# A hybrid decoder layer on one core: projection tiles in the order queries, delta rule, keys, values, pooling, gate, and half of the cached keys multiplied beside the delta rule's tiles

## Chip, cores and metric

One core of a Trainium2 chip. The metric is the device time in microseconds (us) of one execution. Engines: TensorE (PE), VectorE (DVE), ScalarE (ACT), GpSimd (POOL) and SyncE (SP); SP, ACT and POOL also issue DMAs, each in its own program order.

## What is computed

One inference step of a layer with four head groups: A (gated delta rule), B (RWKV-7 time mixing), C (forgetting attention) and D (causal pooling), for a prompt of 1024 tokens and 8 single decode tokens with a cache of 4096 positions each. Cut to its frame:

```python
def _layer(x, start_pos, st, past, P):
    proj = jnp.einsum('ntd,de->nte', x, P['w_in'])
    qkv_A, a_A, b_A, z_A, p_B, z_B, qkv_C, f_C, z_C, u_D, z_D = _split_proj(proj)
    o_A, conv_n, S_A_n = _gdn_branch(qkv_A, a_A, b_A, ...)        # chunks of 64, triangular solve, scan
    o_B, shift_n, S_B_n = _rwkv7_branch(p_B, ...)                 # scan
    o_C, k_n, v_n, lf_n = _fox_branch(qkv_C, f_C, ..., past)      # softmax(q k/8 + decays) v, over the cache too
    o_D, pool_n = _pool_branch(u_D, ...)
    gated = concatenate([o_A*silu(z_A), o_B*silu(z_B), o_C*silu(z_C), o_D*silu(z_D)])
    out = jnp.einsum('nte,ed->ntd', gated, P['w_out'])
    y = _layernorm(ALPHA_DN * x + out, P['ln_g'], P['ln_b'])
```

## The kernel before, in words

**Projection.** The 7,200-odd input columns are cut into 57 tiles of 128 columns. Tile names: MISC; BT (16 tiles of B, the last of each four its gate); AT (16 of A, likewise); CQ, CK, CV, CZ (queries, keys, values, gate of C, four each); DU, DZ (input and gate of D, four each). `self.seq` lists the tiles in the order in which they are multiplied; before it is MISC, BT, AT, CQ, DU, DZ, CK, CV, CZ. `project` computes one tile with 144 matmuls of 344 columns (float32 split in a high and a low part) into three PSUM banks tagged `pj`, of which there are only three, so the next tile starts when ACT has copied the previous one out (`stg<-pj`, L365). Weights arrive by DMA as `raw`; ACT makes `whi`, DVE `wlo`.

**Fillers.** All other work is written as generators. `project` calls `fill` four times for each tile; a call lets every registered generator advance by its rate (counted in `yield`s), and `drain` runs what is left once the tiles are used up. A scheduler with its own cost table then fixes the order of instructions on every engine; on the chip each engine keeps that order.

**Stages.** `inputs` multiplies MISC and BT beside B's preparation, then AT beside A's preparation (`prep_a`, rate 1.6) and `start_b` (triangular inverses of B, decode step of B; rate 1). `inputs_cd` multiplies the last 24 tiles beside two generators:

- `cached` (rate 1.6): inverses of A, `decode_k` (scores of the 8 decode tokens against 32 pages each of cached keys: 64 MB on SP's DMA queue as 256 issues of 256 KB into tiles `dkv`, 1024 small matmuls `k<-dkv,dqb`, L997), and `decode_softmax`.
- `recurrent` (rate 1.0): `chain_b` and `chain_a` (16 chunks each, one `yield` a chunk), then, once the last DZ tile is there, `branch_d` (8 yields), `post_chain_b` (16 yields), then, once the cached softmax and the last CK tile are done, `setup_late` (constants, read through a tile `late` of the stage pool) and `c_first`: for attention heads 1 and 0 it loads queries and keys and finds the row maxima of the scores (`c_max`: 12 matmuls `a<-ckx,cqm` with a mask each, 12 DVE reductions `cmx<-a` into 8 columns, L785 to L799; the maxima go through a small DMA `cmr<-cml` back to partitions of `cqx`, L832).

The pool `stage2` of `inputs_cd` has two buffers `stg`. A CZ tile uses both: one for the projected tile, one as scratch for its silu (L1204 to L1212, three DVE and three ACT passes of 1032 columns). `branch_d` does a silu of the same size for each of its four groups.

**After the projection** `mixing` runs attention for 8 heads (`s`, `cpt`, `cph`, `cpl`, `v`) with the cached values (`decode_v`) as filler, then the output projection (`o`) and the norm.

Of the kernel before, what the change touches and what calls it, by code (L numbers as in the profile page):

```python
# [17 lines left out]
N = T + NS  # L18
G3 = 344
GROUPS = (392, 384, 256)  # L20
RATE_R = 1.0
EARLY = (1,)
RATE_P = 1
SPOOL = {0: 99, 1: 99, 2: 0}
# [15 lines left out]
MISC, CQ, CK, CV, CZ, DU, DZ, BT, AT = 0, 1, 5, 9, 13, 17, 21, 25, 41  # L40
# [139 lines left out]
class Kernel:  # L180
# [732 lines left out]
        nc.gpsimd.dma_start(self.G[8 + hp, :, :T], num)  # L913


    def pages(self, pool, bufs, lead):

        tiles = {}

        def load(n):  # L920
            t = tiles[n] = self.t(pool, [128, 1024], "dkv", bufs=bufs)
            c, b = divmod(n, 8)
            src, view = self.I["ck"], t.rearrange("p (j h k) -> p j (h k)", j=2, h=4)
            for j in range(2):
                v = self.page(32 * b + 2 * c + j, src.shape[0])
                s = src[bass.ds(v, 1)].rearrange("a p h k -> (a p) (h k)")
                self.paged.append(self.nc.sync.dma_start(view[:, j], s))

        def get(n):
            for m in range(n, min(n + lead + 1, 128)):  # L930
                if m not in tiles:
                    load(m)
            return tiles[n]
        return get
# [17 lines left out]
            return tiles[n]  # L952
        return get

    def decode_k(self, **side):


        nc, I, O = self.nc, self.I, self.O
        pj, lf = O["pj"], self.lfd
        with self.tc.tile_pool(name="dqk", bufs=1, **side) as pool:  # L960
            qs = self.t(pool, [128, 4, 8], "dqs")
            nc.gpsimd.dma_start(qs, pj[CQ:CQ + 4, :, T:].rearrange("t p b -> p t b"))
            qb = self.t(pool, [128, 4, 8, 32], "dqb")
            nc.gpsimd.memset(qb, 0.0)
            qf = qb.rearrange("p h b m -> p h (b m)")
            for hh in range(2):
                r = slice(64 * hh, 64 * hh + 64)
                nc.vector.tensor_copy(qf[r, :, 8 * hh::33][:, :, 0:8], qs[r])
            get = self.pages(pool, 3, 2)
            get(0)  # L970
            yield True
            carry = None
            for c in range(16):
                if c % 2 == 0:

                    cum = self.t(pool, [128, 1 + 512], "dcum")
                    nc.gpsimd.memset(cum, 0.0)
                    for hp in range(4):
                        for hh in range(2):
                            r = slice(32 * hp + 8 * hh, 32 * hp + 8 * hh + 8)  # L980
                            h = 2 * hp + hh
                            nc.gpsimd.dma_start(cum[r, 1:].rearrange("p (g k) -> p g k", k=128),
                                              lf[:, 2 * c:2 * c + 4, 128 * h:128 * h + 128])
                            if c == 0:
                                nc.gpsimd.dma_start(cum[r, 0:1], O["lf"][h, T:].unsqueeze(1))
                    if c:
                        nc.vector.tensor_copy(cum[:, 0:1], carry)
                    nc.vector.tensor_tensor_scan(cum[:, 1:], self.onec.to_broadcast([128, 512]), cum[:, 1:],
                                                 cum[:, 0:1], ALU.mult, ALU.add)
                    carry = self.t(pool, [128, 1], "dcar", bufs=2)  # L990
                    nc.vector.tensor_copy(carry, cum[:, 512:513])
                    s = self.t(pool, [128, 512], "dso")
                ps = self.ps("k", (128, 256))
                for b in range(8):
                    kt = get(8 * c + b).rearrange("p (j h k) -> p j h k", j=2, h=4)
                    for hp in range(4):
                        nc.tensor.matmul(ps[32 * hp:32 * hp + 32], lhsT=qb[:, hp, b], rhs=kt[:, :, hp],  # L997
                                         start=b == 0, stop=b == 7)
                    if b % 2 and b < 7:
                        yield True  # L1000
                o = 256 * (c % 2)
                nc.vector.scalar_tensor_tensor(s[:, o:o + 256], ps, 0.125, cum[:, o:o + 256], op0=ALU.mult, op1=ALU.add)
                if c % 2:
                    nc.gpsimd.dma_start(self.sco[:, 512 * (c // 2):512 * (c // 2) + 512], s)
                yield True
            while CK + 3 not in self.done:
                yield True

            ks = self.t(pool, [128, 4, 8], "dks")
            nc.gpsimd.dma_start(ks, pj[CK:CK + 4, :, T:].rearrange("t p b -> p t b"))  # L1010
            ps = self.ps("k")
            for hp in range(4):
                for b in range(8):
                    nc.tensor.matmul(ps[32 * hp:32 * hp + 32, 0:1], lhsT=qb[:, hp, b], rhs=ks[:, hp, b:b + 1],
                                     start=b == 0, stop=b == 7)
            s0 = self.t(pool, [128, 1], "ds0")
            nc.scalar.activation(s0, ps[:, 0:1], AF.Copy, scale=0.125)
            nc.gpsimd.dma_start(self.sco[:, 4096:4097], s0)
# [732 lines left out]
    def build(self):  # L1751
        tc, nc = self.tc, self.nc
        P = lambda **k: tc.tile_pool(reuse_waits="tile", **k)
# [14 lines left out]
        w = lambda t: [self.I["w"][t][:, 4 * k:4 * k + 4] for k in range(4)]  # L1768
        four = lambda t: list(range(t, t + 4))
        prep = lambda t: [t + 4 * h + i for h in (0, 1) for i in range(4)] + [t + 8, t + 9, t + 10, t + 12, t + 13, t + 14, t + 11, t + 15]  # L1770
        self.seq = [MISC] + prep(BT) + prep(AT) + four(CQ) + four(DU) + four(DZ) + four(CK) + four(CV) + four(CZ)
        with P(name="const", bufs=1) as cp, P(name="psum", bufs=2, space=PSUM) as self.psum0:
            with P(name="psum1", bufs=2, space=PSUM) as self.psum1:
                with P(name="w", bufs=2) as wp, P(name="x", bufs=1) as xp:
# [16 lines left out]
            with P(name="psum2", bufs=2, space=PSUM) as self.psum1:  # L1791
                R = dict(side="right")
                with P(name="wo", bufs=2, **R) as wp, P(name="ost", bufs=2, **R) as sp, P(name="y", bufs=1, **R) as yp, \
# [4 lines left out]
                    with P(name="g1", bufs=1) as g1:  # L1798
                        g = [self.gated(3, g1, sp)]
                        with P(name="posta", bufs=1) as pp:  # L1800
                            post = self.post_chain_a(pp)
# [18 lines left out]
    def inputs(self, cp, sp):  # L1820

        P = lambda **k: self.tc.tile_pool(reuse_waits="tile", **k)
        R = dict(side="right")
        raw = self.post_raw(sp)
        ps = [[self.ps(x, (128, G3)) for x in y] for y in (("pj",) * 3, "aab")]
        self.first(self.seq[0:2], ps)
        with self.tc.high_priority(offset=AHEAD):
            raw(MISC, ps[0])()
        lx = self.lora_inputs(sp)
        with P(name="rows", bufs=1, **R) as rp:  # L1830
            self.rows(rp)
        with P(name="bprep", bufs=1, **R) as bp:
            pb = self.post_b(sp, bp, 1.6)
            with self.tc.high_priority(offset=AHEAD):
                pb(self.seq[1], ps[1])
            self.lora(cp, bp, *lx)
            for t in self.seq[2:17]:
                self.project(t, raw if (t - BT) % 4 == 3 else pb)
            self.drain()
        with P(name="aprep", bufs=1, **R) as ap:  # L1840
            self.decay_columns(sp)
            self.cached_gates(sp)
            pa = self.post_a(sp, ap, 1.6)
            self.add(self.start_b(), 1)
            for t in self.seq[17:33]:
                self.project(t, raw if (t - AT) % 4 == 3 else pa)
            self.drain()

    def inputs_cd(self, sp):
        R = dict(side="right")  # L1850
        raw = self.post_raw(sp)
        self.stage2 = sp
        self.add(self.cached(), RATE_L)
        self.add(self.recurrent(**R), RATE_R)
        for t in self.seq[33:]:
            self.project(t, raw)
        self.drain()

    def start_b(self):

        yield from self.inverses("B")
        with self.tc.tile_pool(reuse_waits="tile", name="smpB", bufs=1) as pool:
            yield from self.sample_b(pool)

    def cached(self):
        yield from self.inverses("A")
        self.done.add("invA")
        while CQ + 3 not in self.done:
            yield 1
        yield from self.decode_k()  # L1870
        yield from self.decode_softmax()
        self.done.add("decK")

# [18 lines left out]
    def recurrent(self, **side):  # L1892

        P = lambda **k: self.tc.tile_pool(reuse_waits="tile", bufs=1, **side, **k)
        yield from self.chain_b(**side)
        while "invA" not in self.done:
            yield 1
        yield from self.chain_a(**side)
        while DZ + 3 not in self.done:
            yield True  # L1900
        with P(name="d") as pool:
            yield from self.branch_d(pool)
        with P(name="post") as pool:
            yield from self.post_chain_b(pool)
        while "decK" not in self.done or CK + 3 not in self.done:
            yield 1
        self.c0 = self.tc.tile_pool(reuse_waits="tile", name="c0", bufs=1, **side)
        pool = self.c0.__enter__()
# [24 lines left out]
```

## Time and profile before

| | us |
|---|---|
| median of three runs (2424.43 to 2431.7) | 2431.46 |
| the profiled execution | 2431.75 |
| its span, first to last instruction | 2430.0 |
| PE busy in the span | 2330.0 (96%) |
| DVE busy | 1371.7 (56%) |
| ACT busy | 940.3 (39%) |

The table's last rows are sums over stages that are limited by different things, so they say little alone; the rows further down are cut by stage. In these, "PEclk" is the share of TensorE's full clock that was granted, and idle time of an engine has behind it what ended it.

### The profile page before, as it was taken

How to read it: one execution, taken by the hardware profiler on the slowest of the kernel's cores; microseconds unless marked ns; L12 is line 12 of the kernel's file. 1: busy time of each engine (PE TensorE's matmuls, PEld its weight loads, DVE VectorE, ACT ScalarE, POOL GpSimd, SP SyncE). 2: the span in 40 equal slices, each digit the busy share in tenths (PEclk: the TensorE clock that was granted, in tenths of full speed). 3: DMA queues.
4: the chain of work that ended last, by engine and by line, in shares of the span. 5: the costliest groups of instructions: out<-in, count | busy, mean ns of one | idle time of the engine just before them, and what ended most of it. 6: DMA issues, size and time to landing. Idle time of an engine off the chain costs nothing. (4 is left out here: it accounts for less than half of the span.)

```text
span 2430.0 us, 48607 instructions
## 1 busy us (share of the span) xinstructions
PE 2330.0 (96%) x18324; PEld 2055.6 (85%) x18324; DVE 1371.7 (56%) x2677; ACT 940.3 (39%) x1861; POOL 298.8 (12%) x416
## 2 busy tenths in 40 slices
PE   8999999999999999999999999999999989999984
PEld 8999999999988999897777777999855579878984
DVE  4665667777465567522222244554588654564598
ACT  5644445434443444221111122553466665201244
POOL 0000000000000000112112111100122110100175
PEclk9999999999999999999999999999999999999997
DMA  6233433545432345878888888553398785783312
GB/s 215 52 107 88 111 87 93 150 92 111 109 79 66 92 105 127 181 191 259 268 266 280 278 282 300 187 159 79 111 277 240 230 299 161 216 299 116 91 65 87
DMA packets 368388, 401.46 MB, mean 165 GB/s; under 512 B 203853, under 2 KB 227326, under 8 KB 367386
## 3 DMA queue, kind: packets, MB, share of 16 engines
q1 hardware_dynamic: 306418, 262.78, 36.8%
q10 hardware_dynamic: 50056, 101.60, 14.9%
q0 software_dynamic: 11680, 33.99, 4.1%
q8 instruction: 144, 2.36, 0.4%
q14 instruction: 90, 0.74, 0.1%
HBM read 314.56 MB, written 83.62 MB: 164 GB/s over the span
## 5 line engine op out<-in xcount | busy, mean ns | idle before, releaser
L308 PE MATMUL pj<-xh,wlo 128*128 128x344 f32 x2688 | 875.2, 327 | 9.6 <-DVE wlo L303 8.2
L309 PE MATMUL pj<-xl,whi 128*128 128x344 f32 x2688 | 871.6, 324 | 0.0
L310 PE MATMUL pj<-xh,whi 128*128 128x344 f32 x2688 | 867.1, 324 | 0.0
L308 PEld LDWEIGHTS pj<-xh,wlo 128*128 128x128 f32 x2688 | 508.9, 189 | 38.2 <-issue 18.6
L309 PEld LDWEIGHTS pj<-xl,whi 128*128 128x128 f32 x2688 | 509.5, 190 | 19.0 <-issue 13.6
L310 PEld LDWEIGHTS pj<-xh,whi 128*128 128x128 f32 x2688 | 508.6, 190 | 16.7 <-issue 13.4
L302 ACT CAST whi<-raw 128x256 fp32r<-128x256 f32 (+1 forms) x504 | 213.0, 424 | 751.8 <-PE pj L310 515.6
L303 DVE TENSOR_TENSOR wlo<-raw,whi 128x256 fp32r<-128x256 f32 (+1 forms) x504 | 224.6, 448 | 393.0 <-ACT whi L302 380.3
L308 PE MATMUL o<-gh,wlo 128*128 128x344 f32 x576 | 184.9, 325 | 3.2 <-ACT gh L1662 2.6
L309 PE MATMUL o<-gl,whi 128*128 128x344 f32 x576 | 187.0, 325 | 0.0
L310 PE MATMUL o<-gh,whi 128*128 128x344 f32 x576 | 186.5, 324 | 0.0
L308 PEld LDWEIGHTS o<-gh,wlo 128*128 128x128 f32 x576 | 108.2, 189 | 26.1 <-DVE y L1687 8.5
L309 PEld LDWEIGHTS o<-gl,whi 128*128 128x128 f32 x576 | 109.6, 190 | 3.9 <-issue 2.5
L310 PEld LDWEIGHTS o<-gh,whi 128*128 128x128 f32 x576 | 109.8, 191 | 3.3 <-issue 3.3
L365 ACT ACTIVATE stg<-pj 128x344 f32<-128x344 f32 x168 | 74.7, 457 | 90.2 <-PE pj L310 89.1
L997 PE MATMUL k<-dkv,dqb 128*32 128x256 f32 x1024 | 90.6, 394 | 13.4 <-DMA dkv<-in_ck 12.9
L1687 DVE TENSOR_TENSOR y<-y,o 128x344 f32<-128x344 f32 x96 | 48.3, 509 | 68.0 <-PE o L310 67.8
L861 DVE TENSOR_TENSOR cpl<-cpt,cph 128x512 fp32r<-128x512 f32 (+1 forms) x96 | 61.7, 660 | 16.2 <-ACT cph L860 15.4
L1105 PE MATMUL k<-dkv,dpT 128*8 128x512 f32 x512 | 69.8, 621 | 0.4 <-DMA dkv<-in_cv 0.4
L308 PE MATMUL o<-gh,wkl 128*128 128x392 f32 (+2 forms) x192 | 63.8, 332 | 0.3 <-DVE wkl L303 0.2
L310 PE MATMUL o<-gh,wkh 128*128 128x392 f32 (+2 forms) x192 | 63.6, 331 | 0.0
L309 PE MATMUL o<-gl,wkh 128*128 128x392 f32 (+2 forms) x192 | 63.3, 330 | 0.0
(594 smaller groups left out, 3405.9 us busy)
## 6 DMA issues: line engine op xcount, KB each, us to landing
dkv<-in_ck SPq DMA_DIRECT2D x256, 256.0 KB
dkv<-in_cv SPq DMA_DIRECT2D x256, 256.0 KB
raw<-in_w ACTq DMA_DIRECT2D x228, 256.0 KB
out_pj<-stg ACTq DMA_DIRECT2D x33, 516.0 KB
bop<-bop SPq DMA_DIRECT2D x16, 1024.0 KB
raw<-in_wo ACTq DMA_DIRECT2D x64, 256.0 KB
aop<-aop SPq DMA_DIRECT2D x16, 768.0 KB
aop<-aost SPq DMA_DIRECT2D x40, 256.0 KB
```

The costliest lines, as they stand in the source:

```text
L302: nc.scalar.copy(hi, raw)
L303: nc.vector.tensor_tensor(lo, raw, hi.bitcast(F32), op=ALU.subtract)
L308: nc.tensor.matmul(ps, lhsT=wlo, rhs=xh, start=start, stop=False)
L309: nc.tensor.matmul(ps, lhsT=whi, rhs=xl, start=False, stop=False)
L310: self.last = nc.tensor.matmul(ps, lhsT=whi, rhs=xh, start=False, stop=stop).ins
L365: self.nc.scalar.activation(dst[:, g * G3:g * G3 + G3], ps[g], func)
L861: nc.vector.tensor_tensor(pl[:, off:], pt[:, off:], ph[:, off:].bitcast(F32), op=ALU.subtract)
L997: nc.tensor.matmul(ps[32 * hp:32 * hp + 32], lhsT=qb[:, hp, b], rhs=kt[:, :, hp], start=b == 0, stop=b == 7)
L1105: mm = lambda i: nc.tensor.matmul(po[32 * i:32 * i + 8], lhsT=pTv[:, c, :, 4 * bg + i], rhs=t[i // 2][:, i % 2], start=False, stop=c == 31)
L1687: nc.vector.tensor_tensor(y[:, s], y[:, s], ps[g], op=ALU.add)
```

## The change

The order of tiles becomes MISC, BT, CQ, AT, CK, CV, DU, DZ, CZ. The four CQ tiles and all AT tiles now run with `start_b`, which gets the first half of `decode_k` behind the decode step of B (`decode_k(0, 8)`; the running sum `carry` is kept in a constant tile). `cached` does the second half, `decode_k(8, 16)`. `inputs_cd` is left with 20 tiles. `recurrent` advances at 1.2 instead of 1.0, and `post_chain_b` stands ahead of the wait for DZ and of `branch_d`.

```diff
-RATE_R = 1.0
+RATE_R = 1.2
...
-    def decode_k(self, **side):
+    def decode_k(self, first, last, **side):
...
-            get = self.pages(pool, 3, 2)
-            get(0)
+            get = self.pages(pool, 3, 2, 8 * last)
+            get(8 * first)
             yield True
-            carry = None
-            for c in range(16):
+            carry = self.carry
+            for c in range(first, last):
...
+            if last < 16:
+                return
             while CK + 3 not in self.done:
                 yield True
...
-        self.seq = [MISC] + prep(BT) + prep(AT) + four(CQ) + four(DU) + four(DZ) + four(CK) + four(CV) + four(CZ)
+        self.seq = [MISC] + prep(BT) + four(CQ) + prep(AT) + four(CK) + four(CV) + four(DU) + four(DZ) + four(CZ)
...
-            self.add(self.start_b(), 1)
-            for t in self.seq[17:33]:
-                self.project(t, raw if (t - AT) % 4 == 3 else pa)
+            self.add(self.start_b(cp), 1)
+            for t in self.seq[17:37]:
+                self.project(t, raw if t < AT or (t - AT) % 4 == 3 else pa)
             self.drain()
...
-        for t in self.seq[33:]:
+        for t in self.seq[37:]:
             self.project(t, raw)
         self.drain()
...
             yield from self.sample_b(pool)
+        self.carry = self.t(keep, [128, 1], "dcar")
+        while CQ + 3 not in self.done:
+            yield 1
+        yield from self.decode_k(0, 8)
 
     def cached(self):
         yield from self.inverses("A")
         self.done.add("invA")
-        while CQ + 3 not in self.done:
-            yield 1
-        yield from self.decode_k()
+        yield from self.decode_k(8, 16)
         yield from self.decode_softmax()
         self.done.add("decK")
...
         yield from self.chain_a(**side)
+        with P(name="post") as pool:
+            yield from self.post_chain_b(pool)
         while DZ + 3 not in self.done:
             yield True
         with P(name="d") as pool:
             yield from self.branch_d(pool)
-        with P(name="post") as pool:
-            yield from self.post_chain_b(pool)
         while "decK" not in self.done or CK + 3 not in self.done:
             yield 1
```

The change as the engines see it, at three places. **First, PE, where the projection ends.** Before, the last matmul `pj` is followed by the score matmuls `s` of head 0:

```order
L310 MATMUL pj_21303<-xh_28_129,whi_21410 128x344
L849 MATMUL s_21543<-cqq_20793,ckk_20792 128x512
L850 MATMUL s_21543<-cqx_20794,ckx_20783 128x512
L855 LDWEIGHTS identb_20156
L855 MATMUL s_21543<-mk_20160,identb_20156 128x128
```

In the changed kernel, at the same place:

```order
L310 MATMUL pj_21199<-xh_28_129,whi_21322 128x344
L745 MATMUL a_21364<-cst_210,cvt_21362 128x128 x4
L785 MATMUL a_21441<-ckx_21423,cqm_21424 128x256
L788 LDWEIGHTS identb_20883
L788 MATMUL a_21441<-mq_20885,identb_20883 128x128
L785 MATMUL a_21445<-ckx_21423,cqm_21424 128x256
```

All 12 maximum matmuls of head 0 (two of them shown) now stand behind the last `pj`, and the first `s` behind them.

**Second, ACT and PE at the border of the last two tiles (CZ+2 and CZ+3).** On ACT, before, only weight casts and weight loads stand directly ahead of the copy of CZ+2 out of PSUM:

```order
L302 CAST whi_21207<-raw_21134 128x256
L302 CAST whi_21236<-raw_21134 128x256
L292 DMA raw_21240<-in_w 128x512
L302 CAST whi_21260<-raw_21187 128x256
L365 ACTIVATE stg_21282<-pj_21074 128x344
```

In the changed kernel the copy of the same tile stands behind the loads of heads 1 and 0 (`cqm`, `ckx`, `cqq`) and behind the silu of the tile before (`stg_20957`):

```order
L302 CAST whi_21200<-raw_21076 128x256
L292 DMA raw_21204<-in_w 128x512
L767 CAST cqm_20893<-cqr_20891 64x1024
L1206 ACTIVATE stg_20957<-stg_20957 128x1032
L769 CAST ckx_20892<-ckr_20890 68x1024
L1207 ACTIVATE stg_20957<-stg_20957,epsone_235 128x1032
L823 CAST cqq_21433<-cqr_21422 128x1024
L1209 ACTIVATE stg_20957<-stg_20957 128x1032
L365 ACTIVATE stg_21171<-pj_20969 128x344
```

On PE, in the changed kernel, between the last matmul of CZ+2 and the first of CZ+3 stand the last product of pooling (`b<-da,dpw`) and five maximum matmuls of head 1, of which two are shown (before, two maximum matmuls stood at this border and no product of pooling):

```order
L310 MATMUL pj_20971<-xh_28_129,whi_21072 128x344
L724 MATMUL b_20824<-da_20802,dpw_20385 128x344
L785 MATMUL a_20903<-ckx_20892,cqm_20893 128x256
L788 LDWEIGHTS identb_20883
L788 MATMUL a_20903<-mq_20885,identb_20883 128x128
L785 MATMUL a_20965<-ckx_20892,cqm_20893 128x256
```

On DVE, in the changed kernel, these stand from the constants of `setup_late` (three rows further up is the last result of pooling, L725 with `b_20824`) to the third pass of the silu of CZ+1 (L1213; line numbers here are one higher than before, so L1205 and L1208 are L1204 and L1207 of before):

```order
L261 MEMSET mk_20887 128x128
L262 CAST mk_20887<-stg_20879 128x128
L768 CAST cqm_20893<-onec_223 2x1024
L737 CAST cvh_21307<-onec_223 128x8x64
L738 TENSOR_SCALAR cvl_21308<-onec_223 128x8x64
L1205 SCALAR_TENSOR_TENSOR stg_20957<-stg_20953 128x1032
L789 TENSOR_REDUCE cmx_20901<-a_20903 128x1
L1208 SCALAR_TENSOR_TENSOR stg_20957<-stg_20953,stg_20957 128x1032
L789 TENSOR_REDUCE cmx_20901<-a_20965 128x1
L789 TENSOR_REDUCE cmx_20901<-a_21018 128x1
L1213 TENSOR_TENSOR stg_20953<-stg_20953,stg_20957 128x1032
```

The pool has two buffers: the scratch tile of this silu (`stg_20957`) needs the one that the constants (`stg_20879`) leave, and the copy of CZ+2 (`stg_21171`) the one that the silu leaves.

**Third, PE beside the delta rule's tiles.** In the changed kernel, in an AT tile, two pages of cached keys (`k<-dkv,dqb`) stand next to a transpose of A's preparation (`a<-cst,am`); before, no row with `dkv` stands anywhere in the AT tiles:

```order
L310 MATMUL pj_10397<-xh_24_125,whi_10518 128x344
L996 MATMUL k_10314<-dkv_10564,dqb_8254 32x256 x4
L996 MATMUL k_10314<-dkv_10589,dqb_8254 32x256 x4
L463 MATMUL a_10739<-cst_210,am_1479_10494 64x64 x3
L1505 MATMUL b_10616<-hsl_10618,bonesr_219 128x512
L1506 MATMUL b_10616<-hsh_10617,bonesr_219 128x512
L463 MATMUL a_10739<-cst_210,am_1479_10494 64x64 x13
L308 MATMUL pj_10395<-xh_25_126,wlo_10543 128x344
```

## Rows read from the trace of the kernel before

**Rows 1.** Page, busy time of each engine in the span.

```profile
span 2430.0 us, 48607 instructions
## 1 busy us (share of the span) xinstructions
PE 2330.0 (96%) x18324; PEld 2055.6 (85%) x18324; DVE 1371.7 (56%) x2677; ACT 940.3 (39%) x1861; POOL 298.8 (12%) x416
```

**Rows 2.** Windows by stage: from:to, length, busy of each engine, PEclk, DMA share, GB/s.

```profile
447.00:915.00 468.00, 463.52 (x3876) 431.29 (x3875) 298.74 (x631) 205.44 (x412) 15.49 (x35) 0.98 0.42 100
915.00:1535.00 620.00, 601.48 (x6509) 498.89 (x6509) 228.73 (x509) 127.87 (x279) 101.02 (x183) 0.99 0.81 243
1535.00:1746.00 211.00, 209.50 (x1379) 204.51 (x1379) 105.74 (x195) 90.06 (x181) 18.39 (x31) 1.00 0.40 120
1746.00:1946.00 200.00, 178.99 (x998) 106.56 (x996) 154.62 (x267) 131.25 (x257) 48.94 (x35) 0.94 0.85 253
```

**Rows 3.** PE's waits, 960 to 1746: us in total, times, longest.

```profile
PE k L997 <- DMA dkv<-in_ck: 12.9, 13, 2.8
```

**Rows 4.** Short windows around three clock falls, columns as in rows 2.

```profile
1136.00:1144.00 8.00, 7.01 (x58) 4.90 (x58) 1.35 (x4) 0.73 (x2) 1.23 (x2) 0.79 0.63 190
1178.00:1190.00 12.00, 10.58 (x90) 7.18 (x94) 2.72 (x5) 1.10 (x3) 0.75 (x2) 0.72 0.68 212
1410.00:1418.00 8.00, 7.44 (x45) 6.44 (x46) 4.71 (x6) 4.04 (x5) 0.64 (x2) 0.79 0.69 205
```

**Rows 5.** Timeline of PE at the projection's end: start, us, instruction.

```profile
1745.87 0.32 PE L310 MATMUL pj<-xh,whi 128*128 128x344 f32 x1
...
1754.23 0.80 PE L868 MATMUL v<-cph,cvl 128*128 128x512 f32 x1
```

**Rows 6.** Timeline of DVE there; in brackets idle before, and what ended it.

```profile
1730.98 0.28 DVE L799 TENSOR_TENSOR cml<-cmt,cmh 8x128 fp32r<-8x128 f32 x1
...
1733.68 0.42 DVE L832 CAST cqx<-cmr 4x512 fp32r<-4x512 f32 x1 [0.59 <-DMA cmr<-cml]
...
1753.81 0.23 DVE L1076 TENSOR_SCALAR dpw<-cst,ds 128x8 f32<-128x8 f32 x1 [0.78 <-DMA ds<-sco]
```

**Rows 7.** Groups by form, DVE, 1620 to 1746: count, busy us, mean ns, idle before.

```profile
L789 DVE TENSOR_REDUCE cmx<-a 128x1 f32<-128x512 f32 x12 | 8.3, 691 | 14.5 <-PE a L785 11.9 <-PE a L788 2.5
L1207 DVE SCALAR_TENSOR_TENSOR stg<-stg,stg 128x1032 f32<-128x1032 f32 x3 | 3.7, 1234 | 5.9 <-ACT stg L1206 5.9
...
L768 DVE CAST cqm<-onec 2x1024 fp32r<-2x1024 f32 x4 | 2.7, 684 | 5.1 <-PE pj L310 5.0
...
L789 DVE TENSOR_REDUCE cmx<-a 128x1 f32<-128x384 f32 x4 | 2.2, 552 | 2.8 <-PE a L788 2.8
L789 DVE TENSOR_REDUCE cmx<-a 128x1 f32<-128x256 f32 x4 | 1.7, 420 | 1.6 <-PE a L788 1.6
...
L824 DVE TENSOR_TENSOR cqx<-cqr,cqm 64x1024 fp32r<-64x1024 f32 x1 | 1.2, 1218 | 0.0
L789 DVE TENSOR_REDUCE cmx<-a 128x1 f32<-128x128 f32 x4 | 1.2, 289 | 4.7 <-PE a L788 4.7
...
L737 DVE CAST cvh<-onec 128x512 fp32r<-128x512 f32 x1 | 0.4, 427 | 0.0
```

**Rows 8.** The same for ACT.

```profile
L365 ACT ACTIVATE stg<-pj 128x344 f32<-128x344 f32 x17 | 7.5, 460 | 15.8 <-PE pj L310 15.8
L1206 ACT ACTIVATE stg<-stg,epsone 128x1032 f32<-128x1032 f32 x3 | 3.5, 1157 | 0.1
...
L769 ACT CAST ckx<-ckr 68x1024 fp32r<-68x1024 f32 x2 | 2.1, 1040 | 0.0
```

**Rows 9.** Line 724: ns min/median/max, first and last start.

```profile
L724 PE MATMUL b<-da,dpw x12: 452/452/557, 1438.7 to 1501.6; 128*128 128x344 f32 x12
```

**Rows 10.** Line 725, the same columns.

```profile
L725 DVE SCALAR_TENSOR_TENSOR dz<-b,par,dz x12: 564/569/576, 1422.7 to 1502.0; 128x344 f32<-128x344 f32 x12
```

**Rows 11.** Groups by form, PE, 1620 to 1746.

```profile
L785 PE MATMUL a<-ckx,cqm 66*128 66x512 f32 x12 | 4.6, 398 | 0.0
```

**Rows 12.** PE's waits over the whole span.

```profile
PE pj L308 <- ACT stg L365: 1.3, 3, 0.5
```

More of the change, by code (lines that the diff above doesn't have):

```diff
@@ L913, in c_gate, with pages @@
         nc.gpsimd.dma_start(self.G[8 + hp, :, :T], num)
-    def pages(self, pool, bufs, lead):
+    def pages(self, pool, bufs, lead, end):
         tiles = {}
@@ L929, in get @@
         def get(n):
-            for m in range(n, min(n + lead + 1, 128)):
+            for m in range(n, min(n + lead + 1, end)):
                 if m not in tiles:
@@ L989, in decode_k @@
                                                  cum[:, 0:1], ALU.mult, ALU.add)
-                    carry = self.t(pool, [128, 1], "dcar", bufs=2)
                     nc.vector.tensor_copy(carry, cum[:, 512:513])
@@ L1854, in inputs_cd, with start_b @@
         self.add(self.recurrent(**R), RATE_R)
-        for t in self.seq[33:]:
+        for t in self.seq[37:]:
             self.project(t, raw)
         self.drain()
-    def start_b(self):
+    def start_b(self, keep):
         yield from self.inverses("B")
```

## Prediction

> **What bounds the kernel now.** I read the page first: PE is busy for 96% of the span [rows 1], so the question is what PE waits for, stage by stage. The windows by stage answer it [rows 2]. While the AT tiles run (447 to 915) PE idles 468 - 463.5 = 4.5 us and DMA is busy for 0.42. While chains and cached keys run (915 to 1535) it idles 18.5 us and DMA is at 0.81. In the last projection stretch (1535 to 1746) it idles 1.5 us; this stretch is full because row maxima are spread between projection matmuls. In attention (1746 to 1946) it idles 21 us. A second loss is the granted clock: 0.98 over 468 us is 9.4 us, 0.99 over 620 us is 6.2 us. So all that can be won ahead of attention, in the stages that the change touches, is 4.5 + 9.4 + 18.5 + 6.2 + 1.5 = 40 us. The list of waits names the largest piece: 12.9 us in 13 waits for pages of cached keys [rows 3].
>
> The change moves matmuls and removes none, so the sum is made of waits that go and waits that come. It starts from the profiled execution's 2431.75 us (0.3 above the median, span 2430.0).
>
> **The pages.** The second half of the keys keeps its rate of 1.6 for a fill and its place beside the chains, so half of the 12.9 us stays. The first half goes where 100 GB/s were moved [rows 2]. Its 32 MB (64 double pages of 512 KB) take 32 steps of two, so the four fills of eight tiles; at 468/16 = 29 us a tile that is 140 GB/s more, 240 in all, which is what the middle moves now (243) with its waits. So waits there are not excluded; but at rate 1 no fill takes two steps. Bounds 0 and 6.5 us; I take 2.5, nearer to nothing. 12.9 becomes 9: **-4 us**, bounds 0 and -12.9. SP's queue is part of this: page issues now stand between the stores and loads of A's preparation, each of which can hold up the pages behind it, and PE stops at a late page with all projection matmuls queued behind.
>
> **The clock beside the pages.** Three falls lie in that stretch; (1 - 0.79) x 8 + (1 - 0.72) x 12 + (1 - 0.79) x 8 = 6.8 us [rows 4]. Half go with half of the waits: **-3**, bounds 0 and -6.8.
>
> **The inverses of B** now run with nothing of A's preparation beside them. Idle and clock of the whole stage are 4.5 + 9.4 = 13.9 us [rows 2]; but the inverse is a chain through one PSUM bank, which still has only projection matmuls to hide behind. **-2**, bounds +3 and -13.9.
>
> **Rate 1.2** changes how many chunks fall on a tile (4.8 instead of 4), not what a chunk costs; beside it stand projection matmuls as before. **0**, bounds -2 and +3. `post_chain_b` moves into tiles that have no other filler; that is free as long as those tiles last.
>
> **What is late next: pooling and the maxima.** Count the fills. Before, `inputs_cd` had 24 x 4 = 96; at rate 1, 32 chunks end at 32, the wait for DZ at 48, pooling at 56, `post_chain_b` at 72, and the 22 yields of `c_first` at 94: just inside. Now there are 80, DZ ends only at 64, and 8 + 22 yields at 1.2 want 25 fills where 16 are left. About 11 yields, the maxima of head 0, are drained with no projection beside them. That is what the order shows at the end, and it also crowds pooling, four CZ silus and the maxima of head 1 into the last four tiles.
>
> *Border of CZ+2 and CZ+3.* PE has only the three `pj` banks, so it waits for ACT's copy of CZ+2, and by the order this copy waits for the silu of CZ+1, whose scratch buffer it takes; the silu stands on DVE behind pooling's last result, which needs a product that PE does only after CZ+2. From the last `pj` of CZ+2: product 0.45 [rows 9], result 0.57 [rows 10], four small constants (estimate 0.8 together, each under the smallest reduction's 0.29), `cqm` 0.68, two casts of 0.43, first silu pass 1.23 [rows 7]: 4.6. Then ACT pass 1.16, `ckx` 1.04, ACT pass 1.16 [rows 8], DVE pass 1.23, ACT pass 1.16, DVE pass 1.23, copy 0.46: 12.0. Casts of `cqq` and the reductions lie beside. PE has the product and five maxima in it, about 2.3 us with 0.38 for one [rows 11]. It idles about 10 us; before, all waits for these copies together were 1.3 us [rows 12]. **+10**, bounds 7 (loads early, short passes) and 14 (pooling's last product itself late, behind POOL's DMAs).
>
> *The end.* Before, the first `s` follows the last `pj` at 1746.0, and the first product with values starts at 1754.23 [rows 5], 8.2 later. Now DVE meets, between the second and the third reduction of head 0, the operation `dpw` that waits for a load; it landed at 1753.8 [rows 6], 7.8 after the end, and nothing makes it earlier. Behind it: ten reductions, 6 x 0.69 + 2 x 0.55 + 0.42 + 0.29 = 5.9; two silu passes 2.5; `cqx` 1.2; two `cqm` 1.4; one cast 0.4 [rows 7]: 11.4, so 19.4 with `dpw`. Then maximum, transposition and split (estimate 1.3), the DMA `cmr` from 1731.26 to 1733.68, 2.4, and the copy 0.42 [rows 6]: 23.5. Exponential and split (estimate 2.5 from passes of half the length in rows 7 and 8) bring the first product with values to 26. That is 18 later than before; but 12 maximum matmuls, 4.6 us [rows 11], leave the tiles, and the projection ends so much earlier. **+13**, bounds 6 (DVE's other passes find gaps, and attention starts with less to do) and 20 (`cqx` slowed, `cmr` queued behind pages).
>
> What the clock does there: it fell to 0.72 and 0.79 in windows with 0.6 to 1.4 us of idle [rows 4], and attention has 0.94 already [rows 2]. The Trainium skill ("TensorE: Matmul & The Clock Gate", Why this matters for your kernels) says that a longer idle gap sends TensorE back to the half clock. By it the 12 maxima of the end would take 4.6 us more, which gives 2451 if they were on the path; by the rows the reductions, at 0.69 against 0.38, set the pace, and the sum stays. I follow the rows.
>
> **Sum.** 2431.75 - 4 - 3 - 2 + 0 + 10 + 13 = 2445.75, as a median 2445.
>
> **Rivals.** 0.3% (7.3 us) is about what a measurement of this kernel can tell from no change.
>
> 1. *The middle pays for all (faster).* If relief on the DMA queues removed every wait and clock fall of the pages and of the stage of AT, -12.9 - 6.8 - 13.9 = -33.6, against +23 at the end: 2421. It decides when the middle gives more than 30 of the 40 us. For it: DMA at 0.42 beside AT. Against: half of the pages stay where they are, at the same rate. 0.13.
> 2. *The end is given back (no change).* Attention idles 21 us in any case [rows 2]. While PE stands at the end, ACT and DVE finish the last silu and the loads of heads 1 and 2, and pages of values arrive. If 10 of the 23 us return, 2436; it decides from 7 us on. Against: heads after the first are not what the order moves. 0.2.
> 3. *The pages beside the delta rule cost more (slower still).* If one in four of the 64 double pages that moved is late by 1.0 us (12.9/13), that is 16 us instead of 2.5: 2459. It decides from about 10 us of such waits. 0.15.
>
> My own case has 0.52, with 2437 to 2456 of its own. Faster 0.13, same 0.2, slower 0.52 + 0.15 = 0.67. The range takes in the centres of the second and the third rival and leaves out the first's, 0.13, and the far tails: 2427 to 2461.
>
> **What would show it.** In the changed trace: waits of PE for `dkv` near 9 us, at most 2.5 of it beside the AT tiles; an idle of about 10 us between the last two CZ tiles, ended by ACT's copy; from the last `pj` to the first product with values about 26 us, with 12 reductions in it; the projection without these two stalls some 9 to 14 us shorter. I am wrong if the copy of CZ+2 does not wait, if `s` starts within 10 us of the last `pj`, or if 915 to 1535 shrinks by more than 20 us for the same work.

## The result and the profile after

| | before | changed |
|---|---|---|
| median of four runs, us | 2430.9 | 2458.6 (2452.7 to 2459.9) |
| the profiled execution, us | 2431.75 | 2457.97 |
| its span, us | 2430.0 | 2456.2 |

The ratio is 1.0121, with a 95% interval of 1.0100 to 1.0143: slower, as forecast, and inside the range, but by 27.7 us where 14 were forecast.

Busy times in the page of the changed kernel, against [rows 1]:

```profile
span 2456.2 us, 48638 instructions
PE 2332.9 (95%) x18324; PEld 2057.2 (84%) x18324; DVE 1383.6 (56%) x2679; ACT 944.4 (38%) x1861; POOL 299.9 (12%) x418
```

PE does the same 18324 matmuls; it is busy for 2.9 us more and stands for 23.3 us more. Where is read from windows (from:to, length, busy of PE, PEld, DVE, ACT, POOL, PEclk, DMA share, GB/s). First the kernel before: all up to CZ+2, and the three AT tiles in which B's inverses ran:

```profile
0.00:1698.50 1698.50, 1664.44 (x14358) 1511.86 (x14358) 900.21 (x1910) 627.89 (x1275) 135.40 (x263) 0.99 0.56 158
547.60:656.80 109.20, 104.72 (x1173) 100.25 (x1172) 68.20 (x150) 45.97 (x88) 8.70 (x17) 0.92 0.55 116
```

Then the changed kernel: up to CZ+2, the four tiles of the same inverses, the tile CZ+2 with the border behind it, and the stretch from the last `pj` to the first product with values:

```profile
0.00:1673.50 1673.50, 1648.13 (x14313) 1502.39 (x14313) 875.61 (x1859) 617.40 (x1260) 127.68 (x249) 0.99 0.54 157
523.10:634.70 111.60, 111.60 (x1090) 107.48 (x1089) 54.58 (x140) 32.07 (x69) 8.62 (x18) 1.00 0.43 94
1673.50:1717.40 43.90, 29.99 (x164) 26.14 (x162) 27.56 (x46) 15.86 (x23) 4.81 (x13) 0.85 0.41 124
1744.40:1778.00 33.60, 12.66 (x44) 7.64 (x43) 23.08 (x35) 13.45 (x18) 8.62 (x6) 0.56 0.73 200
```

Up to CZ+2 the changed kernel is 25.0 us ahead: 8.7 us less idle (34.1 against 25.4), 45 matmuls fewer (37 of them score maxima and what goes with them, the others products of pooling; all come later now), and less time at the lower clock. Then it loses 13.9 us of idle at one border and 20.9 after the last `pj` (5.6 before).

The border, in PE's timeline (start, us, instruction, in brackets idle before it and what ended it):

```profile
1699.70 0.31 PE L310 MATMUL pj<-xh,whi 128*128 128x344 f32 x1
1704.44 1.52 PE L724 MATMUL b<-da,dpw 128*128 128x344 f32 x2 [4.42 <-DVE dz L725]
1712.20 0.58 PE L785 MATMUL a<-ckx,cqm 66*128 66x256 f32 x1 [6.25 <-ACT ckx L769]
...
1717.38 0.66 PE L308 MATMUL pj<-xh,wlo 128*128 128x344 f32 x1 [1.05 <-ACT stg L365]
```

17.4 us pass between the last matmul of CZ+2 and the first of CZ+3. PE waits first for pooling, then for the loads of head 1, and only for the last 1.05 us for ACT's copy. Two products of pooling stand here behind the last `pj`; the order shown ahead of the prediction has one.

The end, PE first, as in [rows 5]:

```profile
1744.04 0.32 PE L310 MATMUL pj<-xh,whi 128*128 128x344 f32 x1
...
1774.31 0.79 PE L850 MATMUL s<-cqx,ckx 68*128 68x512 f32 x1 [6.03 <-DVE cqx L832]
...
1778.04 0.78 PE L868 MATMUL v<-cph,cvl 128*128 128x512 f32 x1
```

The first product with values starts 33.7 us after the end of the projection (8.0 before, [rows 5]), at 1778.0 instead of 1754.2. DVE in the same stretch, against [rows 6]:

```profile
1752.78 0.23 DVE L1077 TENSOR_SCALAR dpw<-cst,ds 128x8 f32<-128x8 f32 x1 [1.70 <-DMA ds<-sco]
...
1759.79 1.23 DVE L1213 TENSOR_TENSOR stg<-stg,stg 128x1032 f32<-128x1032 f32 x1 [2.18 <-ACT stg L1209]
...
1766.14 0.69 DVE L789 TENSOR_REDUCE cmx<-a 128x1 f32<-128x512 f32 x1
1766.87 0.17 DVE L792 TENSOR_TENSOR cm<-cmx 128x8 f32<-128x8 f32 x1
1767.80 1.99 DVE L798 CAST cmh<-cmt 8x128 fp32r<-8x128 f32 x1 [0.77 <-ACT cmt L796]
1769.83 1.12 DVE L799 TENSOR_TENSOR cml<-cmt,cmh 8x128 fp32r<-8x128 f32 x1
1773.84 0.42 DVE L832 CAST cqx<-cmr 4x512 fp32r<-4x512 f32 x1 [2.89 <-DMA cmr<-cml]
```

This is the chain of the prediction, link by link, and each link is longer than its estimate.

Some of PE's waits over the whole span, against [rows 3] and [rows 12] (us in total, times, longest):

```profile
PE a L785 <- DVE cmx L789: 13.1, 7, 3.3
PE k L996 <- DMA dkv<-in_ck: 8.7, 9, 3.3
PE a L785 <- ACT ckx L769: 6.2, 1, 6.2
PE s L850 <- DVE cqx L832: 6.0, 1, 6.0
PE b L724 <- DVE dz L725: 5.9, 2, 4.4
PE pj L308 <- ACT stg L365: 3.1, 5, 1.1
```

Pooling's results in the changed kernel (count, ns min/median/max, first to last start), against [rows 10]:

```profile
L725 DVE SCALAR_TENSOR_TENSOR dz<-b,par,dz x12: 565/570/576, 1637.9 to 1706.0; 128x344 f32<-128x344 f32 x12
```

Pooling takes 68 us from first to last result, 79 before. It begins when DZ+3 leaves PSUM, at 1624.5, and so ends at 1706.6, in the last tile but one.

### The profile page after: what moved, and what is told of

The parts are those of the page before. It is cut to its first block, busy times and chain, and to the rows that moved or that the text cites. A ratio compares the mean times of both kernels' runs of the same rounds, so it can differ in the third digit from the quotient of the medians.

```text
span 2456.2 us, 48638 instructions
## 1 busy us (share of the span) xinstructions
PE 2332.9 (95%) x18324; PEld 2057.2 (84%) x18324; DVE 1383.6 (56%) x2679; ACT 944.4 (38%) x1861; POOL 299.9 (12%) x418
## 5 line engine op out<-in xcount | busy, mean ns | idle before, releaser
L308 PEld LDWEIGHTS pj<-xh,wlo 128*128 128x128 f32 x2688 | 507.0, 189 | 41.1 <-issue 13.9
L309 PEld LDWEIGHTS pj<-xl,whi 128*128 128x128 f32 x2688 | 507.7, 189 | 13.1 <-issue 8.2
L310 PEld LDWEIGHTS pj<-xh,whi 128*128 128x128 f32 x2688 | 506.9, 189 | 13.1 <-issue 9.8
L861 DVE TENSOR_TENSOR cpl<-cpt,cph 128x512 fp32r<-128x512 f32 (+1 forms) x96 | 67.4, 720 | 13.8 <-ACT cph L860 13.0
```

What stands on the lines that cost most here:

```text
L308: nc.tensor.matmul(ps, lhsT=wlo, rhs=xh, start=start, stop=False)
L309: nc.tensor.matmul(ps, lhsT=whi, rhs=xl, start=False, stop=False)
L310: self.last = nc.tensor.matmul(ps, lhsT=whi, rhs=xh, start=False, stop=stop).ins
L861: nc.vector.tensor_tensor(pl[:, off:], pt[:, off:], ph[:, off:].bitcast(F32), op=ALU.subtract)
```

## The experiments

Each is compared with the kernel before, run on the same chip (its median lay between 2429.4 and 2431.7 us there). `v` is the start of the first product with values in the run's profile, which is one execution (its time, in the fourth column, lies up to 12 us from the median). From `v` to the end of the span it is 673 to 698 us, so `v` shows what a run lost ahead of attention, and not all of its time.

| run | median us | ratio (95%) | profiled us | last `pj` starts | `v` |
|---|---|---|---|---|---|
| before | 2430.9 | | 2431.75 | 1745.9 | 1754.2 |
| changed | 2458.6 | 1.0100 to 1.0143 | 2457.97 | 1744.0 | 1778.0 |
| e_nosplit | 2461.0 | 1.0108 to 1.0153 | 2455.86 | 1744.1 | 1776.6 |
| e_order_only | 2456.0 | 1.0071 to 1.0153 | 2453.46 | 1741.2 | 1774.2 |
| e_keys_only | 2517.5 | 1.0331 to 1.0382 | 2520.62 | 1724.3 | 1830.5 |
| e_cq_only | 2489.9 | 1.0223 to 1.0284 | 2488.74 | 1782.6 | 1810.2 |
| e_split_only | 2477.7 | 1.0171 to 1.0230 | 2466.46 | 1763.7 | 1791.8 |
| e_rate10 | 2462.4 | 1.0066 to 1.0168 | 2464.68 | 1727.1 | 1775.8 |
| e_late2 | 2456.8 | 1.0089 to 1.0132 | 2449.34 | 1727.3 | 1772.9 |
| e_split_late2 | 2469.0 | 1.0097 to 1.0205 | 2469.95 | 1722.3 | 1780.9 |
| e_no_pool | 2431.6 | 0.9975 to 1.0016 | 2443.95 | 1723.7 | 1744.3 |
| e_dfirst | 2488.4 | 1.0218 to 1.0265 | 2488.28 | 1781.1 | 1809.1 |
| e_dmid | 2482.2 | 1.0176 to 1.0229 | 2486.89 | 1779.6 | 1808.3 |
| e_one | 2454.8 | 1.0086 to 1.0144 | 2448.71 | 1735.2 | 1762.2 |
| e_two | 2470.5 | 1.0148 to 1.0201 | 2470.65 | 1766.2 | 1793.3 |
| e_brate | 2439.7 | 1.0012 to 1.0048 | 2442.99 | 1750.1 | 1758.0 |
| e_chainb | 2505.2 | 1.0239 to 1.0347 | 2515.51 | 1820.4 | 1828.4 |

**First four: is it the place of pooling, or the keys?**

e_dfirst, the changed kernel with one line changed (e_dmid has CK, DU, DZ, CV there):

```diff
-        self.seq = [MISC] + prep(BT) + four(CQ) + prep(AT) + four(CK) + four(CV) + four(DU) + four(DZ) + four(CZ)
+        self.seq = [MISC] + prep(BT) + four(CQ) + prep(AT) + four(DU) + four(DZ) + four(CK) + four(CV) + four(CZ)
```

> The changed kernel with one edit: the tiles DU, DZ stand ahead of CK, CV again (queries, delta rule, pooling input, pooling gate, keys, values, gate); the half of the keys beside the delta rule's tiles, the rate 1.2 and the place of post_chain_b stay. Theory: the change pays at two places only, both because pooling and the row maxima come too late (in its trace 17.4 us pass between the last projection matmul of CZ+2 and the first of CZ+3, and the first product with values comes 33.7 us after the last projection matmul instead of 8.2), and the middle is some 14 us faster than before. Then this kernel ends near 2431 - 14 = 2417 us (2410 to 2425), with under 4 us of idle at the border of CZ+2 and the first product with values within 15 us of the last projection matmul. Rival (the halves of the keys and the 20 instead of 24 tiles are what costs): 2445 or more.

> The changed kernel with the values' tiles CV behind DZ (queries, delta rule, keys, pooling input, pooling gate, values, gate). By the count of fills pooling ends after tile 50 and the maxima of the first head after tile 52, one tile later than with pooling ahead of the keys, but the cached keys' softmax ends three tiles earlier. Theory as for the kernel with pooling ahead of keys: 2417 us (2410 to 2427), border idle under 4 us, first product with values within 15 us of the last projection matmul. Rival (keys beside the delta rule cost): 2445 or more.

Both missed, far to the other side: 2488.4 and 2482.2. With `post_chain_b` ahead of it, pooling begins only at 1640 in e_dfirst, although DZ has been there since 1372. Its products and the first maxima stand on PE ahead of CZ+2, and PE idles for 40.1 of the 78.1 us of the tile CZ+1. Two of PE's waits in e_dfirst:

```profile
PE b L724 <- DVE dz L725: 20.4, 3, 10.3
PE s L850 <- DVE cqx L832: 9.2, 1, 9.2
```

So the order of tiles alone does not place pooling; its place in the row of work of `recurrent` counts too.

e_late2, a buffer of its own for the constants (`self.late` is taken once, from a pool beside `stage2`):

```diff
-        late = self.t(stage, [128, 4 + N], "stg")[:, 0:NLATE]
+        late = self.late
```

> The changed kernel with one edit: the constants of setup_late get a buffer of their own instead of one of the two stg buffers, so that the copy of CZ+2 no longer hangs behind them. In its order of instructions the copy stands ahead of the silu of CZ+1, and 22 of the 24 maximum matmuls of the first two heads come behind the last projection matmul instead of 12. Theory (two separate prices): the border's 17 us fall to under 4, but some ten more maxima at the end cost 6 to 12 us there, so 2445 to 2455 us. Rival (the wait at the border is for pooling's last product, not for the buffer): border idle stays over 8 us and the time is 2458 or more.

The border is nearly gone (one wait of 4.6 us), the projection ends 17 us earlier, 22 of the 24 maxima come behind it, and the time is 2456.8: no measurable difference from the changed kernel. In this pair border and end are thus one price, paid in either place.

e_nosplit, no keys beside AT (the first three lines go from `start_b`, the others are in `cached`):

```diff
-        while CQ + 3 not in self.done:
-            yield 1
-        yield from self.decode_k(0, 8)
...
-        yield from self.decode_k(8, 16)
+        yield from self.decode_k(0, 16)
```

> The changed kernel with one edit: no cached keys beside the delta rule's tiles; all 16 rounds of decode_k run in the last 20 tiles at rate 1.6. Theory (the split relieves the middle): PE's waits for dkv go back to 12 us or more and the clock falls with them, while border and end stay, so 2463 to 2475 us. Rival (keys beside the delta rule are what costs): 2440 or less. Third (the split does nothing, the middle is faster for another reason): 2455 to 2462.

The third case: 2461.0, overlapping the changed kernel's interval. PE's waits for keys are what they were with the split:

```profile
PE k L996 <- DMA dkv<-in_ck: 8.7, 10, 2.0
```

**The parts of the change, one at a time.** The four runs that follow start from the kernel before.

e_cq_only moves `four(CQ)` ahead of `prep(AT)` and the first loop to `self.seq[17:37]`, nothing else; e_split_only adds `decode_k(0, 8)` to `start_b`; e_order_only has the rest:

```diff
-RATE_R = 1.0
+RATE_R = 1.2
...
-        self.seq = [MISC] + prep(BT) + prep(AT) + four(CQ) + four(DU) + four(DZ) + four(CK) + four(CV) + four(CZ)
+        self.seq = [MISC] + prep(BT) + prep(AT) + four(CQ) + four(CK) + four(CV) + four(DU) + four(DZ) + four(CZ)
...
+        with P(name="post") as pool:
+            yield from self.post_chain_b(pool)
         while DZ + 3 not in self.done:
...
-        with P(name="post") as pool:
-            yield from self.post_chain_b(pool)
```

> The kernel before with two parts of the change alone: CQ ahead of AT, and half of the cached keys beside AT. Pooling's tiles stand ahead of the keys, pooling ahead of post_chain_b and the rate is 1.0, as before. New theory after the first four runs: with CQ ahead everything behind A's inverses (chains, pooling, post_chain_b, maxima) starts four tiles, some 95 us, later; in the middle 12 us are won because the inverses of B no longer share their tiles with A's preparation; and where post_chain_b stands ahead of pooling, pooling's products hold PE. Here pooling stands first, so 2431 - 12, and 5 to 20 for maxima crowded into the last two tiles: 2424 to 2440 us. Rival (pooling is late in any order once CQ stands ahead): 2465 or more.

> The kernel before with one part of the change alone: CQ ahead of AT. All cached keys stay in the last stage. New theory (the middle's gain comes from B's inverses apart from A's preparation, and splitting the keys gives little): within 5 us of the run that also splits the keys, with PE's waits for dkv no more than 4 us apart. Rival (the split relieves the middle): slower than that run by 8 us or more.

> The kernel before with the rest of the change alone: keys and values ahead of pooling's tiles, post_chain_b ahead of pooling, rate 1.2; CQ stays behind AT and the keys in one piece. Theory (the price at the border and at the end comes from pooling that waits for DZ and from maxima behind it, whether or not the chains start later): 2431 + 17 + 21, about 2468 (2455 to 2480), with 10 us or more of idle at the border of the last two tiles and the first product with values 25 us or more behind the last projection matmul. Rival (the price comes from the four tiles by which CQ delays the chains): 2440 or less.

e_order_only has the whole price, 2456.0, with its chains as early as before: the rival there, 2440 or less, is out. The idle of 10 us or more at the border did not come (0.0 us in the tile CZ+2, 2.5 in CZ+1); the price shows at the end alone, where `v` comes 32.7 us behind the projection. CQ ahead alone costs more than the whole change, 2489.9, and with the split 2477.7, so the forecast of 2424 to 2440 was wrong, and so was that the two lie within 5 us. In e_cq_only chains, pooling and `post_chain_b` come later; `post_chain_b` and the loads of the maxima then hold PE ahead of CZ+2:

```profile
PE b L1504 <- DVE hsl L1503: 17.6, 7, 4.4
PE a L785 <- ACT ckx L769: 13.4, 1, 13.4
```

The split is worth 12 us in this order (the intervals barely overlap), and nothing measurable in that of the change. In e_split_only pooling ends at 1590.5, 116 us earlier than in the changed kernel, and the time is still 2477.7: late pooling is not the only way to be late.

e_brate has `self.add(self.start_b(), 0.6)`.

> The kernel before with one number changed: start_b (inverses and decode step of B) advances at 0.6 instead of 1 beside AT. Theory (inverses of B and A's preparation in the same tiles cost about 12 us by waits and half clock around 550 to 630): with fewer yields to a tile they spread, and 3 to 10 us of it are won: 2421 to 2428. Rival (the 12 us come only with tiles that hold nothing else): 2429 to 2434.

2439.7, slower by 0.12 to 0.48%: a miss. The first inverses still share AT+4 with A's preparation (43.1 us for that tile, 41.1 before), and B's decode step runs on until the chains begin. The three tiles from AT+4 on together took 95.4 us, against 109.2 before, and the last DZ tile is through 18.0 us earlier; five tiles further on the run is 2.2 us behind. From the end of DZ to 1600 us PE waits 10.9 us for keys, 1.7 before. What the middle won was lost again ahead of the end.

**What pooling, buffers and rate cost.**

In e_no_pool `branch_d` gives way to copies, e_split_late2 is e_split_only with the buffer of e_late2, e_rate10 has `RATE_R = 1.0`, and in e_chainb the line `yield from self.chain_b()` moves to the end of `start_b` in the kernel before, with `bufs=1` for `bop`.

> The changed kernel without the work of pooling: branch_d is replaced by four copies of query tiles into its output rows, and its state output is a copy of its input, so that nothing waits for DZ (24 products, about 4 us of PE, are left out too). Theory (pooling behind DZ is what delays the maxima, and border and end are the whole price): 2458.6 - 17 - 21 - 4, about 2417 us (2408 to 2428), first product with values within 15 us of the last projection matmul. Rival (chains and post_chain_b, four tiles late, are enough by themselves): 2440 or more.

> The run with CQ ahead of AT and the split alone (2478 us, with 31 us of idle of PE in the tile CZ+1), with one edit more: the constants of setup_late get a buffer of their own. Theory (the two stg buffers tie the projection to the constants, and these to the end of pooling and post_chain_b): the 31 us of idle fall to under 6, the 24 maxima move behind the last projection matmul and cost 10 to 20 us there: 2456 to 2468. Rival (PE stands because the work itself is late): 2473 or more.

> The changed kernel with the rate of recurrent back at 1.0. In its order of instructions all 24 maximum matmuls of the first two heads stand behind the last projection matmul (12 in the changed kernel). Theory (a chunk costs the same at either rate, and maxima behind the projection cost 0.5 to 1 us each): the middle stays, 2455 to 2470 in all, up to the border of CZ+2 no more than 3 us from the changed kernel. Rival (1.2 crowds the chains and costs there): 2450 or less.

> The kernel before with chain_b (16 chunks) taken out of recurrent and run behind B's decode step beside the last AT tiles; one buffer instead of two for its operands, to fit the memory. Cached keys, order of tiles and rates are those of before. Theory (what helps is a shorter serial chain behind A's inverses, and less beside the tiles with 46 to 50 us): 2416 to 2428. Rival 1 (the same work costs the same elsewhere): 2428 to 2434. Rival 2 (chain_b beside A's preparation collides on DVE): 2436 or more.

Without pooling's work `v` starts at 1744.3 and the time is 2431.6, between theory (2417) and rival (2440): 27 us come back, a part of them work left out. PE still waits once, 15.4 us, for `cqx`. The profiled execution is the slowest of eleven, 2443.95: `v` is 9.9 us earlier than before, and what follows is longer at a lower clock. This is the stretch from `v` to the output projection, before, in e_no_pool and in e_one (columns as above):

```profile
1754.20:1946.60 192.40, 176.36 (x983) 104.79 (x981) 147.53 (x259) 125.50 (x246) 44.11 (x33) 0.95 0.85 251
1744.30:1959.30 215.00, 189.75 (x987) 110.00 (x986) 148.81 (x258) 126.50 (x249) 43.93 (x34) 0.90 0.74 217
1762.20:1965.20 203.00, 184.94 (x980) 108.86 (x978) 142.57 (x253) 125.87 (x245) 40.74 (x31) 0.90 0.74 229
```

Why this stretch is longer in some runs is not shown. The own buffer brings e_split_only from 2477.7 to 2469.0 only, with no idle left in CZ+1: most of what PE stood for was late work. The rate is worth nothing that can be measured. e_chainb lost 75 us, 37.7 of them in six waits for its single operand buffer, so it says nothing on the place of `chain_b`.

**The last three.** e_keys_only is e_order_only without the swap of `post_chain_b` and without the rate. e_one and e_two have one and two tiles of CQ ahead of AT in the kernel before.

> The kernel before with one edit: CK, CV ahead of DU, DZ. Pooling stays ahead of post_chain_b, the rate is 1.0, CQ stays behind AT, keys in one piece. In its order of instructions 19 of the 24 rounds of post_chain_b and all 24 maximum matmuls stand behind the last projection matmul. Theory (all that waits for DZ is pushed towards the end, and putting post_chain_b ahead of pooling was what kept the change's price small): first product with values 80 us or more behind the last projection matmul, 2490 to 2560 in all. Rival (the swap is worth nothing, the price of late pooling is the same 25 us): 2448 to 2465.

> The kernel before with one tile of CQ (instead of four) ahead of AT, nothing else. Theory (before, the maxima of the first head end 23 us ahead of the last projection matmul, so a delay of the chains by one tile, 23 us, just fits, while a part of the 12 us of B's inverses is won): 2422 to 2431. Rival (each tile ahead of AT is paid at the end, 58 us for four): 2440 to 2450.

> The same with two tiles of CQ ahead of AT. Theory (the delay, 45 us, is more than the 23 us of slack): 10 to 30 us slower than with one tile, 2435 to 2460. Rival (the price comes only where four tiles make PE stand in CZ+1): 2431 or less.

2517.5: keys ahead of pooling alone cost 86 us, because `post_chain_b` and the maxima then wait for DZ too; the swap inside the change, with the rate, saves some 60 of them. PE waits in it:

```profile
PE b L1504 <- DVE hsl L1503: 44.0, 11, 9.0
```

One tile of CQ ahead of AT costs 24 us, two 40, four 60. My theory of 23 us of slack at the end is wrong: the price starts with the first tile. In the profile of e_one `v` comes 8.0 us later, and another 10.6 come in the stretch behind it (the third row above). No run is faster than the kernel before.

## Why the prediction was right in sign and half in size

**What bounds the kernel** held: PE is full in the middle, and what counts is what comes late.

**Pages, -4.** Their waits fell from 12.9 to 8.7 us as forecast, but the split is not shown to be the reason: without the split they are 8.7 too. In the runs with all keys beside the chains they lie between 8.7 (e_nosplit) and 16.8 us (e_brate), so a change of 4 us is within what these waits vary by. Rival 3 gave 2459, nearly the measured time, for the wrong reason: the waits did not grow.

**Clock, -3**, did not come. Up to CZ+2 both kernels show 0.99, but from the end of the AT tiles on (915 us before, 1015.5 now) it is 0.99 before and 0.98 now. What was won in clock was won beside the inverses of B.

**Inverses of B, -2**, was mis-sized. In the three tiles that they shared with A's preparation PE had 4.5 us of idle and a PEclk of 0.92 (0.08 x 109 = 8.7 us); in their four tiles of the changed kernel 0 us and 1.00. That is some 13 us, near the bound of -13.9. In e_order_only, which keeps the shared tiles, the same three took 6.7 us less than in the profile of before, so the gain is between 6 and 13.

**Rate 1.2, 0**, held: e_rate10 reaches CZ+2 at 1673.8, the changed kernel at 1673.5.

**Border, +10**, was mis-sized: 17.4 us from `pj` to `pj` where I had 12.0 to the copy's end. From pooling's last result (1706.6) to the copy's end (1717.3) it is 10.7, for which I had 11.0. The rest, 5.5, is the result itself: I let it come 1.0 us after the last `pj` of CZ+2, and it came 6.6 after. Of the 17.4 us PE idles 12.4, inside the bound of 14; the other 5.0 are the products and the five maxima, for which I had 2.3. Those figures were from rows at the full clock; from 1673.5 to 1717.4 PEclk is 0.85, and the sum has no term for that.

Behind the 5.5 us lies the step "count the fills". It took pooling as 8 yields of a fill's time, 41 us at 4.8 yields and 24.5 us a tile. But pooling is a chain of loads, adds and a silu for each of its four groups, of 79 us between first and last result already before [rows 10], and 82 us from the copy of DZ+3 here. I had the row and used it for durations only. What the count gave for the end held: 12 maxima are left there.

**Luck.** By the terms the projection should have ended 3.6 us earlier (-4 - 3 - 2 + 10, and -4.6 for the maxima that leave); it ended 1.8 earlier. This is not the terms being right: up to CZ+2 the changed kernel was 25.0 us ahead, where the terms without the border give 13.6, and the last two tiles then took 23.2 us more than before, where the border's term gives 10. Part of both is work that moved from one side to the other; the rest are errors that cancel.

**End, +13**, is the step that failed: the first value product at 26 us behind the projection, measured 33.7, which makes the term 21 (25.6 later than before, less the 4.6) instead of 13. The path was the forecast one, but nearly every link on it was too short. Link by link: `dpw` 0.6 later; to the last reduction 13.8 instead of 11.4, because ACT's last silu pass stood behind the loads of the next heads; maximum to split 4.1 instead of 1.3; the small DMA 2.9 instead of 2.4; exponential to product 3.8 instead of 2.5. With the projection's end 1.8 us ahead instead of 3.6, and 2.5 us more behind `v`, that makes 7.7 + 1.8 + 2.5 = 12.0 of the 12.2 us between the sum (2445.75) and the profiled execution (2457.97).

**The reason that the runs give.** What sets the time seems to be when the work of `recurrent` behind the last DZ tile is through: pooling, constants, loads, maxima. With keys and values ahead, that tile leaves PSUM at about 1624 (1615 in e_nosplit, 1639 in e_order_only), and it takes 135 to 161 us more to `v`, whatever the middle has won. e_order_only and e_no_pool show both sides: the order (with swap and rate) has the price, and without pooling's work nearly all of it is gone. It would also explain why CQ ahead costs 60 us alone and nothing measurable in the change: there, the chains' delay lies inside the wait for DZ. That reading fits the runs but none isolates it: e_no_pool leaves out both the wait and the work, and DZ's time alone does not fix `v`, which comes 2.4 us earlier in e_order_only than in e_nosplit though DZ comes 24 us later. Rival 2, 10 of 23 us given back in attention, did not come: behind `v` it took 678.2 us, against 675.8.

**The clock at the end.** The Trainium skill ("TensorE: Matmul & The Clock Gate", Why this matters for your kernels) says that an idle gap between bursts of matmuls takes TensorE back to half of its clock. The trace agrees: PE had waited 2.4 us and stood again, for 3.3 us, when the granted clock fell; it is 1.00 from 1744.4 to 1748.4 and 0.50, the lower of its two levels, from there to 1778.0. But 12.5 of the 13.1 us that PE waits for DVE's reductions lie there, and DVE waits only 0.8 us for the maxima, so the slower matmuls did not set the pace, as forecast. (By the page's rule the prediction's own figures give 2445.75 + 4.6 = 2450, not 2451.)

## What to carry to other kernels

Fillers that are advanced by counts look like quantities; those at the end are chains. Before moving the tile that one of them waits for, add up its own time from first to last result and lay it behind the new place of that tile, and ask what stands behind it in program order. Two stalls on one chain can be one price, as e_late2 shows: take the later event (here the first product with values), not the sum of the waits.

## What was not expected of the hardware

Small DVE operations waited out POOL's. The cast of `cmh`, 8 x 128, took 1.99 us and `cml` 1.12; for the next head, with POOL free, they take 0.21 and 0.27. POOL in the same microseconds:

```profile
1767.36 2.36 POOL L825 TENSOR_TENSOR ckk<-ckr,ckx 64x1024 fp32r<-64x1024 f32 x1
1769.78 1.03 POOL L826 CAST ckk<-ckx 64x1024 fp32r<-64x1024 f32 x1
```

`cmh` ends 0.07 us after the first of these, `cml` 0.14 us after the second. DVE's `cqx` (L824) took 3.17 us at 1747.2 in the same way, and 1.21 at 1763.6 with POOL free. The Trainium skill ("SBUF — State Buffer", Who interferes with whom) says that an operation of VectorE with two inputs in SBUF and one of GpSimd that reads SBUF exclude each other for the whole instruction; the trace agrees for `cml` and `cqx`. It shows the same for the cast `cmh`, which has one input. POOL pays as well: beside `cqx` its cast (L826) took 1.91 us, otherwise 1.03 to 1.38. By these durations some 2.6 us of the end are this (1.99 - 0.21 and 1.12 - 0.27); no run isolates it.
